# Both directions of a delta rule advanced side by side, and conditioning products on four column groups

## The chip, the cores and the metric

One core of a Trainium2 chip runs the whole program in one launch. The metric is the device time of that launch in microseconds (us). PE is TensorE, DVE VectorE, ACT ScalarE, POOL GpSimd, SP SyncE, whose queue issues the loads.

## The reference

Two blocks follow each other, on 512 latent and 256 context tokens of width 1024, in float32. The first block:

```python
mod = silu(c) @ mod_w + mod_b            # likewise for c_ctx: "conditioning"
p = (layer_norm(x) * (1 + sc) + sh) @ w_in
pv, u, fh, g = split(p)
y = rwkv(shift3(u_ctx), shift3(u_lat))   # 6 heads of 64, two directions
o = hgrn(fh_ctx, fh_lat)                 # 6 heads of 64, two directions
mix = concat(pool(pv), y, o) * silu(g)
x = layer_norm(ALPHA * x + gate * (mix @ w_out)) * ln_g + ln_b
```

The delta rule of `rwkv` runs forward and backward over the tokens, the context first, and per token t it computes

```python
sa = S @ kk_t
S = S * w_t - outer(sa, kk_t * a_t) + outer(v_t, k_t)
y_t = S @ r_t                            # latent tokens only; y of both directions is added
```

The second block (a gated delta net, an attention layer, two feed-forward layers) also takes conditioning products, `silu(c_2) @ ada_w_2`, 2 x 6144 columns. The change does not touch the rest of it.

## The kernel before, in words

Data lie feature-major: tiles of 128 features by tokens. Float32 accuracy of the large products comes from splitting both factors in a high and a low part (`dense`, L272: three products each). Tile's scheduler puts every engine's instructions in one fixed order ahead of the run; dense and conditioning products are placed around the serial chains.

`block1` has two parts. In the first (the opening), 8 loads of 384 KB bring x, `layer_norm` takes sums (L344, `mv`), and `ada` computes the first conditioning group (L311, bank `mi`, 12 load buffers). In the second a loop over n in 0 to 5 takes one piece of `rwkv_pair`, one of `hgrn_pair` and a group of `ada` (bank `ma`, 3 load buffers), then gates and the output product follow.

`ada` multiplies 32 condition columns by a group of 2048 weight columns: for each k of 8 and each of nb = 4 blocks b, a 128x512 tile (256 KB, L310) is loaded and multiplied into rows 32b to 32b+31 of one bank (L311). A float32 matmul leaves two records in the trace. 32 such products are in the opening, 208 in the loop (six groups with nb = 4, one with nb = 2).

`rwkv_pair(p)` (p = 0, 1, 2: two heads) projects k, v, r and calls `rwkv_unit(p, dd)` for each direction dd, so six units run one behind the other. A unit prepares decays and scaled keys (L672 to L728), and then goes through its 12 chunks of 64 tokens in two halves of 6. For each half `rwkv_pre` takes scores on PE (L758), masks them on DVE (L761), and inverts unit triangular blocks of 32 by 32 in `inv32`: 15 rounds of shuffle, product and difference on DVE (L831, L832, L833), from L826 to the transpose of L853, with one merge of 16 to 32; then a merge to 64 (L788 to L807). Each of 6 `rwkv_chunk` steps is a chain: products on PE (L865, L866), a copy on ACT (L870), PE (L872), DVE (`uv`, L873), PE (L875), and the state update `rS` on DVE (L877). The decayed state `pe` (L862) is on ACT. Scores `scs`, transposed keys `bkt`, values `uv` and inverse `tt` lie in the pool `f2`, with two buffers, so a half can be prepared while the other's steps run. `rwkv_out` (L892, L893) multiplies out late. HGRN units begin at L987 (`hlf`) on DVE and end at L946 (`hoa`) for every second of them.

Of the kernel before, what the change touches and what calls it, by code (L numbers as in the profile page):

```python
# [192 lines left out]
class B:  # L193
# [108 lines left out]
    def ada(self, s, c0, w, g, nb, out, bias, st="m"):  # L302
# [10 lines left out]
        ev = pool.tile([128, 512], F32, tag="raw", name="adaev", bufs=nr)  # L313
# [106 lines left out]
    def block1(self):  # L420
# [6 lines left out]
        with tc.tile_pool(name="b1a", bufs=2) as pool, self.banks(mv=6, mi=2), self.stream("i", 12, 1):  # L427
# [13 lines left out]
        with ExitStack() as ctx:  # L441
# [23 lines left out]
            self.late, self.last = None, {}  # L465
# [3 lines left out]
            for n in range(6):  # L469
                next(rw, None)  # L470
# [22 lines left out]
            self.late()  # L493
# [118 lines left out]
    def rwkv_pair(self, p):  # L612
# [26 lines left out]
        last = self.late

        def readout():

            last()
# [14 lines left out]
        self.late = readout  # L658

    def rwkv_unit(self, p, dd, r, k, v, kk, y, pb):  # L660

        nc, tc = self.nc, self.tc
        f1 = self.f1
        col = dd * 3 + p
        P64 = slice(64 * dd, 64 * dd + 64)
        th = {}
        for nm, src, up, hb in (("w", self.xw, self.wup, "rwkv_w0"), ("a", self.xa, self.aup, "rwkv_a0")):
            t = f1.tile([128, NT], F32, tag="t" + nm, name="t" + nm)
            for c0, cn in (LAT, CTX):
                o = self.mm()  # L670
                nc.tensor.matmul(o[:, :cn], up[P64, 128 * p:128 * p + 128], src[P64, c0:c0 + cn], start=True, stop=True)
                nc.vector.tensor_scalar(t[:, c0:c0 + cn], o[:, :cn], self.V(hb, col), SIG_MIN, op0=ALU.add, op1=ALU.max)  # L672
            self.sigmoid(t)
            th[nm] = t
        lw, ta = th["w"], th["a"]
        g = f1.tile([128, 12, 64], F32, tag="G", name="G")
        self.cumsum(g.rearrange("p c t -> p (c t)"), lw, 64, dd)
        e = lw.rearrange("p (c t) -> p c t", t=64)
        nc.scalar.activation(e, g, AF.Exp, scale=CDEC)
        nc.scalar.activation(g, g, AF.Exp, scale=-CDEC)  # L680
        en = g
        end = 63 if dd == 0 else 0
        ec = self.f2.tile([128, 12], F32, name="rec")
        nc.gpsimd.tensor_copy(ec, e[:, :, end])
        kkv = kk.rearrange("p (c t) -> p c t", t=64)
        rv = r.rearrange("p (c t) -> p c t", t=64)

        halves = ((0, 1, 2), (3, 4, 5)) if dd == 0 else ((0, 1, 5), (2, 3, 4))
        ars = []
        for cps in halves:  # L690
            ar = self.ar[self.arn % 3]
            self.arn += 1
            ars.append(ar)
            runs = [(2 * cps[0], 6, 0)] if cps[2] - cps[0] == 2 else [(0, 4, 0), (10, 2, 4)]
            for c, n, q in runs:
                for h in range(2):
# [8 lines left out]
                    lo = max(c, 4)
                    if lo < c + n:
                        nc.gpsimd.tensor_tensor(ar[H, q + lo - c:q + n, h, 1, :], e[H, lo:c + n], rv[H, lo - 4:c + n - 4],
                                                op=ALU.mult)

        bk = f1.tile([128, 6, 4, 64], F32, tag="BK", name="BK")  # L710
        km = f1.tile([128, NT], F32, tag="km", name="km")
        nc.vector.tensor_scalar(km, ta, self.V("rwkv_k_a", p), self.ka[:, p:p + 1], op0=ALU.mult, op1=ALU.add)
        nc.vector.tensor_tensor(km, km, k, op=ALU.mult)
        env = en.rearrange("p (c q) t -> p c q t", q=2)
        nc.vector.tensor_tensor(bk[:, :, 0:4:3, :], km.rearrange("p (c q t) -> p c q t", q=2, t=64), env, op=ALU.mult)
        nc.vector.tensor_tensor(ta, ta, kk, op=ALU.mult)

        tav = ta.rearrange("p (c q t) -> p c q t", q=2, t=64)
        for q in range(2):
            nc.vector.tensor_tensor(bk[:, :, 1 + q, :], tav[:, :, q], env[:, :, q], op=ALU.mult)  # L720
        if dd == 0:
            nc.vector.scalar_tensor_tensor(pb, km[:, 256:], self.V("rwkv_r_k", p), r, op0=ALU.mult, op1=ALU.mult)
        else:
            nc.vector.scalar_tensor_tensor(km[:, 256:], km[:, 256:], self.V("rwkv_r_k", 3 + p), r, op0=ALU.mult, op1=ALU.mult)
            nc.gpsimd.tensor_tensor(pb, pb, km[:, 256:], op=ALU.add)
            bs = self.mm()
            nc.tensor.matmul(bs, self.C("bones"), pb, start=True, stop=True)
# [17 lines left out]
    def rwkv_pre(self, cps, dd, bk, ar, v):  # L745
# [30 lines left out]
        if self.late:  # L776
            self.late()
# [938 lines left out]
```

## Time and profile before

| | |
|---|---|
| median of 3 runs | 2768.44 us (2766.35 to 2769.46) |
| the profiled execution | 2766.63 us, span 2764.8 us |
| busy of the span | PE 2609.9 us (94%), DVE 1687.3 (61%), ACT 1294.9 (47%), POOL 290.4 (11%) |
| block 1 | 0 to 876.5 us of the span |
| state updates L877 | 72, from 173.4 to 860.5 us |

A busy share is an average over the span, and PE's ends are modelled, so a busy PE isn't PE at its peak. Times in a window table are counted from the span's start; "PEclk" is the granted clock of TensorE, 1.00 being full speed. Idle time of an engine is put down to what released it last.

### The profile page before, as it was taken

What the parts mean: (1) busy time and instruction counts of PE and PEld (TensorE: products, weight loads), DVE (VectorE), ACT (ScalarE), POOL (GpSimd) and SP (SyncE); (2) the same over time, 40 slices, a digit from 0 to 9 for tenths busy, and PEclk for the clock granted to TensorE, in tenths of its full rate; (3) what the DMA queues carried; (4) which work ended last, traced back from release to release, by engine and by line L of the source; (5) the groups of instructions that cost most, each with busy time, mean ns of one, the idle gap of its engine ahead of it and who ended that gap; (6) DMA issues with size and microseconds to landing.
All of it is one profiled execution on the core that took longest, in us unless ns stands there. A gap on an engine that the chain in (4) does not pass through costs nothing.

```text
span 2764.8 us, 50823 instructions
## 1 busy us (share of the span) xinstructions
PE 2609.9 (94%) x19688; PEld 1987.2 (72%) x19688; DVE 1687.3 (61%) x4379; ACT 1294.9 (47%) x2927; POOL 290.4 (11%) x387
## 2 busy tenths in 40 slices
PE   8999999999988989999889999999998999999998
PEld 3754645564545777777777888888887788888888
DVE  3676576677666657777766444244454677664665
ACT  2454354546455565555444332133344555543444
POOL 0120021012103001111210110011000000010010
PEclk9999999999989999999989999999999999999999
DMA  5234143323434220111131222222231012233225
GB/s 188 77 100 129 58 138 100 116 62 108 135 92 153 81 71 33 35 37 40 61 102 41 68 65 61 62 64 65 76 110 47 28 29 86 81 96 97 98 90 157
DMA packets 130083, 230.91 MB, mean 84 GB/s; under 512 B 14768, under 2 KB 30384, under 8 KB 129840
## 3 DMA queue, kind: packets, MB, share of 16 engines
q1 hardware_dynamic: 129840, 227.65, 26.7%
q8 instruction: 154, 2.52, 0.4%
q14 instruction: 89, 0.73, 0.1%
HBM read 217.90 MB, written 9.70 MB: 82 GB/s over the span
## 4 chain that ended last, share of the span: by engine, by line
PE 46%; DVE 2%; ACT 1%; issue 1%; POOL 1%; DMA 0%; POOLq 0%; DVEq 0%; SPq 0%; ACTq 0%
PE mm L272 39%; PE ms L1670 2%; PE mv L344 1%; PE mt L1689 1%; PE mt L1683 1%; PE mm L1620 1%; PE mf L272 0%; DVE hl L416 0%; DVE ht L414 0%; DVE wlo L259 0%; POOL qr L1604 0%; POOL qr L1603 0%; ACT whi L258 0%; DMA raw<-ffn_up 0%; ACT hh L415 0%
## 5 line engine op out<-in xcount | busy, mean ns | idle before, releaser
L259 DVE TENSOR_TENSOR wlo<-raw,whi 128x512 fp32r<-128x512 f32 (+3 forms) x560 | 387.2, 693 | 368.5 <-ACT whi L258 224.6
L258 ACT CAST whi<-raw 128x512 fp32r<-128x512 f32 (+3 forms) x560 | 331.7, 594 | 467.8 <-PE mm L272 409.5
L272 PE MATMUL mm<-hh,whi 128*128 128x512 f32 (+1 forms) x1960 | 480.4, 358 | 22.6 <-ACT hh L415 13.3
L272 PE MATMUL mm<-hl,whi 128*128 128x512 f32 (+1 forms) x1960 | 456.4, 349 | 0.1
L272 PE MATMUL mm<-hh,wlo 128*128 128x512 f32 (+1 forms) x1960 | 452.1, 348 | 0.4 <-DVE wlo L259 0.4
L272 PEld LDWEIGHTS mm<-hh,whi 128*128 128x128 f32 x1960 | 330.6, 191 | 87.8 <-ACT hh L415 21.2
L272 PEld LDWEIGHTS mm<-hl,whi 128*128 128x128 f32 x1960 | 327.8, 192 | 48.3 <-issue 5.1
L272 PEld LDWEIGHTS mm<-hh,wlo 128*128 128x128 f32 x1960 | 326.5, 192 | 48.1 <-issue 5.4
L311 PE MATMUL ma<-raw,cvs 128*32 128x512 f32 x416 | 178.6, 620 | 8.4 <-DMA raw<-ada_w 7.1
L1168 POOL TENSOR_TENSOR fc<-fc,fc 128x768 f32<-128x768 f32 (+1 forms) x44 | 69.2, 1572 | 867.6 <-DVE fc L582 635.0
L272 PE MATMUL mm<-fh,whi 128*128 128x256 f32 (+1 forms) x616 | 136.2, 340 | 1.0 <-ACT fh L391 1.0
L580 DVE SCALAR_TENSOR_TENSOR fc<-mm,vec,fc 128x511 f32<-128x511 f32 (+1 forms) x132 | 86.8, 658 | 79.9 <-ACT fc L579 79.9
L272 PE MATMUL mm<-fl,whi 128*128 128x256 f32 (+1 forms) x616 | 130.5, 330 | 0.0
L272 PE MATMUL mm<-fh,wlo 128*128 128x256 f32 (+1 forms) x616 | 129.3, 328 | 0.0
L579 ACT ACTIVATE fc<-mm,vec 128x512 f32<-128x512 f32 (+1 forms) x132 | 81.4, 617 | 96.5 <-PE mm L272 96.4
L272 PEld LDWEIGHTS mm<-fh,whi 128*128 128x128 f32 x616 | 99.9, 190 | 15.7 <-issue 3.4
L272 PE MATMUL mf<-hh,whi 128*128 128x512 f32 (+1 forms) x360 | 103.2, 385 | 5.6 <-ACT whi L258 2.9
L1132 DVE SCALAR_TENSOR_TENSOR xr<-mm,m,xr 128x512 f32<-128x512 f32 (+1 forms) x112 | 66.4, 596 | 67.6 <-PE mm L272 67.6
L272 PEld LDWEIGHTS mm<-fl,whi 128*128 128x128 f32 x616 | 99.0, 190 | 11.3 <-issue 0.5
L272 PEld LDWEIGHTS mm<-fh,wlo 128*128 128x128 f32 x616 | 98.6, 190 | 10.5
L272 PE MATMUL mf<-hl,whi 128*128 128x512 f32 (+1 forms) x360 | 96.4, 368 | 0.0
L344 PE MATMUL mv<-sq,con 128*128 128x256 f32 (+1 forms) x240 | 84.9, 453 | 11.9 <-ACT sq L348 11.5
(539 smaller groups left out, 4483.3 us busy)
## 6 DMA issues: line engine op xcount, KB each, us to landing
raw<-ada_w SPq DMA_DIRECT2D x192, 256.0 KB, 3.0
raw<-ffn_up SPq DMA_DIRECT2D x176, 256.0 KB, 2.6
raw<-ffn_down SPq DMA_DIRECT2D x96, 256.0 KB, 2.7
raw<-w_in SPq DMA_DIRECT2D x66, 256.0 KB, 3.0
raw<-ab_w_in SPq DMA_DIRECT2D x50, 256.0 KB, 2.8
raw<-mod_w SPq DMA_DIRECT2D x48, 256.0 KB, 3.8
raw<-ffn_down SPq DMA_DIRECT2D x48, 192.0 KB, 2.4
raw<-w_out SPq DMA_DIRECT2D x32, 256.0 KB, 2.9
```

The source lines that it names most:

```text
L258: nc.scalar.copy(hi[:, :nk], raw[:, :nk])
L259: nc.vector.tensor_tensor(lo[:, :nk], raw[:, :nk], hi[:, :nk].bitcast(F32), op=ALU.subtract)
L272: nc.tensor.matmul(o, a[:, k], b[:, k0 + k, t:e], start=(k0 == 0 and j == 0 and k == 0), stop=(k0 + n == nk and j == 2 and k == n - 1))
L311: nc.tensor.matmul(acc[32 * b:32 * b + 32, :], s[:, k, :], t, start=(k == 0), stop=(k == 7))
L344: self.nc.tensor.matmul(v[:, :x.shape[1]], self.C("ones"), x, start=(k == 0), stop=(k == 7))
L579: nc.scalar.activation(out[:, c0:c0 + cn], o[:, :cn], AF.Copy, scale=w[1])
L580: nc.vector.scalar_tensor_tensor(out[:, c0 + 1:c0 + cn], o[:, :cn - 1], w[0], out[:, c0 + 1:c0 + cn], op0=ALU.mult, op1=ALU.add)
L1132: nc.vector.scalar_tensor_tensor(x, o[:, :cn], gcol(m, 0 if c0 else 1), x, op0=ALU.mult, op1=ALU.add)
L1168: nc.gpsimd.tensor_tensor(g, g, u, op=ALU.mult)
L1620: nc.tensor.matmul(o[:, e], a[:, k, T], b[:, k], start=(i == 0), stop=(i == 5))
L1670: nc.tensor.matmul(o[:, at:at + cn], a, b, start=(j == 0), stop=(j == 4))
L1683: nc.tensor.transpose(tp[:, j], p[:, (c0 + j) * 128:(c0 + j + 1) * 128], self.C("ident"))
```

## The change

1. `ada` goes through its 512 columns in two halves c; per k one load brings 256 columns of all nb blocks (512 KB for nb = 4, in runs of 1 KB where there were 2 KB), and four products of 256 columns, on four column groups, stand next to each other. Load buffers: 6 in the opening instead of 12, still 3 in the loop, of twice the size.
2. `rwkv_unit` is replaced. `rwkv_prep` prepares both directions; then three sets g of 4 chunks per direction follow. `rwkv_pre(g)` takes the scores of both directions; all blocks are inverted by one `inv8` (8 blocks of 32 by 32 in four row groups; direction 0's are transposed so that both have the same triangle): 7 rounds, then two merge levels. `scs`, `bkt` and `uv` move to `f1`, one buffer each; the inverse `tt` is one fixed tile.
3. `rwkv_chunk` makes a step of both directions, 36 in all: `pe` on POOL, products side by side, `uv` on DVE for direction 0 and on ACT for 1, and two updates. `rwkv_out` runs right behind a set.
4. The loop takes two pieces of `rwkv_pair` for even n and one for odd n.

The second block keeps `inv32`. The diff's core:

```diff
     def ada(self, s, c0, w, g, nb, out, bias, st="m"):
...
-        for k in range(8):
-            for b in range(nb):
-                t = pool.tile([128, 512], F32, tag="raw", name="raw", bufs=nr)
-                nc.sync.dma_start(t, w[k * 128:(k + 1) * 128, g * 2048 + b * 512:g * 2048 + b * 512 + 512])
-                nc.tensor.matmul(acc[32 * b:32 * b + 32, :], s[:, k, :], t, start=(k == 0), stop=(k == 7))
+        for c in (0, 256):
+            for k in range(8):
+                t = pool.tile([128, 4, 256], F32, tag="raw", name="raw", bufs=nr)
+                nc.sync.dma_start(t[:, :nb], w[k * 128:(k + 1) * 128, g * 2048:g * 2048 + nb * 512]
+                                  .rearrange("p (b n) -> p b n", b=nb)[:, :, c:c + 256])
+                for b in range(nb):
+                    nc.tensor.matmul(acc[32 * b:32 * b + 32, c:c + 256], s[:, k, :], t[:, b], start=(k == 0), stop=(k == 7))
...
-        with tc.tile_pool(name="b1a", bufs=2) as pool, self.banks(mv=6, mi=2), self.stream("i", 12, 1):
+        with tc.tile_pool(name="b1a", bufs=2) as pool, self.banks(mv=6, mi=2), self.stream("i", 6, 1):
...
             for n in range(6):
-                next(rw, None)
+                for _ in range(2 - n % 2):
+                    next(rw, None)
                 next(hg)
...
+        bk, ec = self.rwkv_prep(p, r, k, v, kk, pb)
+        yield
...
+        for g in range(3):
+            pre = self.rwkv_pre(g, bk, v)
+            sts = []
+            for i in range(4):
+                sts.append(st)
+                st = self.rwkv_chunk(g, i, ec[:, :, 4 * g + i], pre, st)
+            if g:
+                self.rwkv_out(g, sts, pre, y)
...
+        scs = f1.tile([128, 2, 2, 2, 2, na, 64], F32, tag="scs", name="scs", padded_shape=[128, 2, 2, 2, 2, 2, 64])
+        bkt = f1.tile([128, 2, 2, 2, 128], F32, name="bkt")
+        uv = f1.tile([128, 2, 2, 2, 128], F32, name="uv")
...
+    def inv8(self, c32, U):
...
+        nc.vector.tensor_tensor(x, c32, bc("d8"), op=ALU.mult)
+        for n, o in zip(("o8", "o16"), offs):
+            nc.gpsimd.tensor_tensor(o, c32, bc(n), op=ALU.mult)
...
+        for j in range(7, 0, -1):
+            W = slice(j, 8)
+            nc.vector.stream_shuffle(sh[:, :, W], x8[:, :, W], [8 * b + j for b in range(4) for _ in range(8)])
+            nc.vector.tensor_tensor(pr[:, :, W], sh[:, :, W], a[:, :, j:j + 1].broadcast_to([128, U, 8 - j]), op=ALU.mult)
+            nc.vector.tensor_tensor(x8[:, :, W], x8[:, :, W], pr[:, :, W], op=ALU.subtract)
...
+        for o in offs:
+            nc.vector.transpose(flat(t), flat(x))
...
+                        nc.tensor.matmul(ps[R, n, u], l[R, u], r[R, u], start=True, stop=True, tile_position=(32 * i, 32 * i))
...
+            nc.vector.tensor_tensor(x, x, ps[:, 1], op=ALU.subtract)
...
+    def rwkv_chunk(self, g, i, ec, pre, st):
...
+        nc.gpsimd.tensor_tensor(pe, st, ec.rearrange("p (d o) -> p d o", o=1).broadcast_to([128, 2, 64]), op=ALU.mult)
         ch = self.psum("rch", (128, 4, 128))
...
+            for dd, j, q, b in at:
+                nc.tensor.matmul(ch[b, 0, H[h]], scs[:, dd, j, q, h, 0], uv[:, dd, j, q, H[h]], start=True, stop=False)
+            for dd, j, q, b in at:
+                nc.tensor.matmul(ch[b, 0, H[h]], self.ar[g][dd][:, 2 * j + q, h, 0], st[:, dd], start=False, stop=True)
...
+            if dd == 0:
+                nc.vector.tensor_scalar(uv[b, dd, j, q], ch[b, 1], -1.0, None, op0=ALU.mult)
+            else:
+                nc.scalar.activation(uv[b, dd, j, q], ch[b, 1], AF.Copy, scale=-1.0)
...
+            nc.vector.scalar_tensor_tensor(st2[:, dd], ch[:, 2, H[dd]], ec[:, dd:dd + 1], pe[:, dd], op0=ALU.mult, op1=ALU.add)
```

How the change moves instructions, at three places. First PE at its start, where `mv` are the sums of layer norm and `mi` the conditioning products, before:

```order
L344 MATMUL mv<-x_92,con 128x512 x8
L311 MATMUL mi<-raw,cvs 32x512 x3
L344 MATMUL mv<-sq,con 128x512
L311 MATMUL mi<-raw,cvs 32x512
L344 MATMUL mv<-sq,con 128x512
L311 MATMUL mi<-raw,cvs 32x512 x2
L344 MATMUL mv<-sq,con 128x512
L311 MATMUL mi<-raw,cvs 32x512
```

and now:

```order
L351 MATMUL mv<-x_92,con 128x512 x8
L318 MATMUL mi<-raw,cvs 32x256 x4
L351 MATMUL mv<-sq,con 128x512
L318 MATMUL mi<-raw,cvs 32x256 x4
L351 MATMUL mv<-sq,con 128x512
L318 MATMUL mi<-raw,cvs 32x256 x4
L351 MATMUL mv<-sq,con 128x512 x2
L318 MATMUL mi<-raw,cvs 32x256 x4
```

Lone products and pairs have become sets of four of half the width, each behind a product of the sums.

Second DVE in the second head pair of the program before, where one half's inverse (`rx`, `rpr`, `rsh`) meets the other's steps (`uv`, `rS`):

```order
L831 STREAM_SHUFFLE rsh<-rx_4500 128x6x5
L832 TENSOR_TENSOR rpr<-rsh,ra_4499 128x6x5
L833 TENSOR_TENSOR rx_4500<-rx_4500,rpr 128x6x5
L831 STREAM_SHUFFLE rsh<-rx_4500 128x6x6
L832 TENSOR_TENSOR rpr<-rsh,ra_4499 128x6x6
L833 TENSOR_TENSOR rx_4500<-rx_4500,rpr 128x6x6
L873 TENSOR_SCALAR uv<-rch 64x128
L831 STREAM_SHUFFLE rsh<-rx_4500 128x6x7
L832 TENSOR_TENSOR rpr<-rsh,ra_4499 128x6x7
L877 SCALAR_TENSOR_TENSOR rS<-rch,rec,pe 128x64
L833 TENSOR_TENSOR rx_4500<-rx_4500,rpr 128x6x7
```

and now, at the end of one inverse:

```order
L846 STREAM_SHUFFLE rsh<-rx_2815 128x8x7
L847 TENSOR_TENSOR rpr<-rsh,ra_2814 128x8x7
L848 TENSOR_TENSOR rx_2815<-rx_2815,rpr 128x8x7
L849 TENSOR_TENSOR rx_2809<-rx_2815,con_382 128x256
L854 STREAM_TRANSPOSE rt_2810<-rx_2809 128x256
L846 STREAM_SHUFFLE rsh<-rx_4277 128x8
L864 TENSOR_TENSOR rx_2809<-rx_2809,rsc 128x256
L854 STREAM_TRANSPOSE rt_2810<-rx_2809 128x256
L321 COPY adaev<-ma 128x512
L327 TENSOR_TENSOR m_70<-ma,vec 128x16 x2
L864 TENSOR_TENSOR rx_2809<-rx_2809,rsc 128x256
L865 STREAM_TRANSPOSE rt_2810<-rx_2809 128x256
```

The steps are gone from between the rounds; the rounds end with merge levels that wait for PE (`rsc`).

Third DVE at the last steps of the last head pair and the start of the last HGRN unit (`hlf`, `hg`, `hlv`), before:

```order
L831 STREAM_SHUFFLE rsh<-rx_9225 128x6x8
L873 TENSOR_SCALAR uv<-rch 64x128
L832 TENSOR_TENSOR rpr<-rsh,ra_9224 128x6x8
L987 SCALAR_TENSOR_TENSOR hlf<-hz,hg 128x768
L877 SCALAR_TENSOR_TENSOR rS<-rch,rec,pe 128x64
L833 TENSOR_TENSOR rx_9225<-rx_9225,rpr 128x6x8
L593 SCALAR_TENSOR_TENSOR hg<-con,hlf 128x128
L831 STREAM_SHUFFLE rsh<-rx_9225 128x6x9
L593 SCALAR_TENSOR_TENSOR hg<-con,hlf 128x128
L832 TENSOR_TENSOR rpr<-rsh,ra_9224 128x6x9
```

and now:

```order
L937 TENSOR_SCALAR uv<-rch 64x128
L945 SCALAR_TENSOR_TENSOR rS<-rch,rec,pe 128x64 x2
L937 TENSOR_SCALAR uv<-rch 64x128
L945 SCALAR_TENSOR_TENSOR rS<-rch,rec,pe 128x64 x2
L399 TENSOR_TENSOR hl<-gb,hh 128x512 x2
L937 TENSOR_SCALAR uv<-rch 64x128
L1052 SCALAR_TENSOR_TENSOR hlf<-hz,hg 128x768
L945 SCALAR_TENSOR_TENSOR rS<-rch,rec,pe 128x64 x2
L596 SCALAR_TENSOR_TENSOR hg<-con,hlf 128x128 x6
```

The last HGRN unit stood ahead of 10 of the last unit's updates, and stands now ahead of those of two steps.

## Rows read from the trace of the kernel before

**Rows 1.** Windows of the span: window, its length, busy us (records) of PE, PEld, DVE, ACT, POOL, PEclk, DMA share, GB/s.

```profile
0.00:58.00 58.00, 47.73 (x132) 15.04 (x132) 11.69 (x26) 15.04 (x27) 2.45 (x11) 0.99 0.65 220
58.00:173.50 115.50, 105.21 (x608) 76.30 (x609) 81.36 (x218) 60.56 (x115) 20.46 (x35) 0.93 0.24 78
173.50:860.50 687.00, 647.05 (x7546) 362.75 (x7545) 469.30 (x1700) 347.43 (x1117) 97.08 (x186) 0.98 0.35 105
860.50:876.50 16.00, 8.21 (x144) 3.79 (x143) 8.58 (x20) 8.10 (x30) 4.62 (x4) 0.89 0.67 217
876.50:2764.80 1888.30, 1801.72 (x11260) 1529.33 (x11260) 1116.35 (x2418) 863.75 (x1640) 165.83 (x151) 0.98 0.23 71
```

**Rows 2.** Windows by steps and gaps, and idle time ahead of L877, by its releaser.

```profile
173.50:199.50 26.00, 25.74 (x155) 12.98 (x154) 17.70 (x73) 10.79 (x26) 4.36 (x5) 1.00 0.41 132
199.50:219.50 20.00, 14.86 (x319) 9.70 (x317) 16.11 (x64) 11.19 (x45) 3.65 (x10) 0.74 0.11 28
...
307.50:317.80 10.30, 10.30 (x193) 7.74 (x194) 4.17 (x14) 4.28 (x11) 0.83 (x2) 1.00 0.17 53
...
337.50:440.00 102.50, 96.27 (x969) 47.03 (x968) 78.33 (x242) 62.04 (x179) 20.52 (x37) 1.00 0.41 124
...
622.80:693.20 70.40, 63.74 (x871) 34.74 (x867) 56.08 (x198) 45.02 (x151) 14.88 (x24) 0.98 0.35 110
...
842.90:860.60 17.70, 16.76 (x369) 11.22 (x361) 14.62 (x44) 11.58 (x48) 3.49 (x5) 1.00 0.21 62
...
L877 DVE SCALAR_TENSOR_TENSOR rS<-rch,rec,pe x72: 267/283/285, 173.4 to 860.5; 128x64 f32<-128x64 f32 x72
...
  PE rch L875: 19.0, 29
```

**Rows 3.** Lines L826 and L853 (start and end of an inverse): first and last start.

```profile
L826 DVE TENSOR_SCALAR ra<-rc,con x12: 253/631/643, 141.4 to 802.8; 128x96 f32<-128x96 f32 x12
...
L853 DVE STREAM_TRANSPOSE rt<-rx x12: 359/378/379, 164.4 to 833.3; 128x192 f32<-128x192 f32 x12
```

**Rows 4.** Timeline of DVE: two rounds' shuffles; lines of DVE, 58 to 877 us: preparation.

```profile
449.34 0.20 DVE L831 STREAM_SHUFFLE rsh<-rx 128x30 f32<-128x30 f32 x1
...
450.04 0.20 DVE L831 STREAM_SHUFFLE rsh<-rx 128x36 f32<-128x36 f32 x1
...
L593 DVE TENSOR_TENSOR_SCAN G<-con,tw 128x64 f32<-128x64 f32 x72 | 14.7, 269 | 1.7 <-ACT tw L332 1.6
...
L713 DVE TENSOR_TENSOR km<-km,rk 128x768 f32<-128x768 f32 x6 | 5.7, 950 | 0.1
```

**Rows 5.** Windows, line L311 alone (PE, PEld); a PE line of 60 to 890 us.

```profile
0.00:58.00 58.00, 20.78 (x64) 2.91 (x64) 0.99 0.65 220
58.00:877.00 819.00, 178.59 (x416) 23.65 (x416) 0.97 0.34 103
...
L865 PE MATMUL rch<-uv,scs 128*64 128x64 f32 x288 | 40.7, 235 | 1.0 <-DVE rS L877 1.0
```

**Rows 6.** Timeline of PE in the opening: start, length, records.

```profile
25.34 1.04 PE L311 MATMUL mi<-raw,cvs 128*32 128x512 f32 x2
...
27.37 1.06 PE L311 MATMUL mi<-raw,cvs 128*32 128x512 f32 x6
...
52.20 1.90 PE L311 MATMUL mi<-raw,cvs 128*32 128x512 f32 x10
```

**Rows 7.** DMA from 868 to 886 us, GB/s in 40 slices.

```profile
GB/s 0 86 50 237 360 400 405 419 405 405 423 396 387 391 362 373 346 348 350 344 357 357 371 387 387 387 391 178 18 0 0 91 323 314 323 155 155 314 146 178
```

**Rows 8.** Line L987, the start of an HGRN unit.

```profile
L987 DVE SCALAR_TENSOR_TENSOR hlf<-hz,hg x6: 937/945/959, 186.1 to 811.6; 128x768 f32<-128x768 f32 x6
```

**Rows 9.** Timelines of POOL and of DVE around 461 us.

```profile
460.72 1.01 POOL L707 TENSOR_TENSOR AR<-tw,rr 64x384 f32<-64x384 f32 x1 [0.88 <-PE rsc L892]
...
460.76 1.06 DVE L832 TENSOR_TENSOR rpr<-rsh,ra 128x72 f32<-128x72 f32 x1
...
462.42 0.24 DVE L832 TENSOR_TENSOR rpr<-rsh,ra 128x78 f32<-128x78 f32 x1
```

More of the change, by code (lines that the diff above doesn't have):

```diff
@@ L656, in readout, with rwkv_prep @@
                 nc.sync.dma_start(self.ymix[:, 2 + p], y)
-        self.late = readout
-    def rwkv_unit(self, p, dd, r, k, v, kk, y, pb):
-        nc, tc = self.nc, self.tc
+        readout()
+    def rwkv_prep(self, p, r, k, v, kk, pb):
+        nc = self.nc
         f1 = self.f1
[L664 to L684, printed above, removed]
@@ L705, in rwkv_unit @@
[L705 to L713, printed above, removed]
@@ L714, in rwkv_unit @@
[L714 to L718, printed above, removed]
-        for q in range(2):
[L720 to L727, printed above, removed]
-            nc.vector.tensor_tensor(pb, bs, v[:, 256:], op=ALU.mult)
@@ new lines, in rwkv_pre @@
+        Q = [slice(32 * i, 32 * i + 32) for i in range(4)]
+        quads = [(dd, slice(4 - 4 * dd, 8 - 4 * dd), 2 * b + dd, 2 * b + 1 - dd, *((x, t) if dd == 0 else (t, x)))
+                 for dd in range(2) for b in range(2)]
+        for u in range(4):
+            for dd, U, s, e, x_, t_ in quads:
+                nc.tensor.matmul(ps[Q[e], 0, U.start + u],
+                                 scs[Q[s], dd, u // 2, 1 - s // 2, u % 2, 0, 32 * (e % 2):32 * (e % 2) + 32],
+                                 t_[Q[s], U.start + u], start=True, stop=True, tile_position=(32 * s, 32 * e))
@@ new lines, in rwkv_pre @@
+        for dd, U, s, e, x_, t_ in quads:
+            (nc.vector.tensor_copy if s > 1 else nc.scalar.copy)(w[Q[e], U], ps[Q[e], 0, U])
+        for u in range(4):
+            for dd, U, s, e, x_, t_ in quads:
+                nc.tensor.matmul(ps[Q[s], 1, U.start + u], w[Q[e], U.start + u], x_[Q[e], U.start + u],
+                                 start=True, stop=True, tile_position=(32 * e, 32 * s))
+        for dd, U, s, e, x_, t_ in quads:
+            q = 1 - s // 2
+            for z in (s, e):
+                nc.scalar.copy(tt[Q[z], U, q, 32 * (z % 2):32 * (z % 2) + 32], x_[Q[z], U])
@@ new lines, in rwkv_chunk @@
+        xs = self.f1.tile([128, 128], F32, name="xs", bufs=2)
+        nc.scalar.copy(xs, ch[:, 0])
+        for h in range(2):
+            for dd, j, q, b in at:
+                nc.tensor.matmul(ch[b, 1, H[h]], self.tt[:, 4 - 4 * dd + 2 * j + h, q], xs[:, H[h]], start=True, stop=True)
+        for dd, j, q, b in at:
+            if dd == 0:
+                nc.vector.tensor_scalar(uv[b, dd, j, q], ch[b, 1], -1.0, None, op0=ALU.mult)
+            else:
+                nc.scalar.activation(uv[b, dd, j, q], ch[b, 1], AF.Copy, scale=-1.0)
@@ L899, in rwkv_out @@
-        return emit
+                    nc.tensor.matmul(yp[H, T], st[:, dd], self.ar[g][dd][:, 2 * j + q, h, 1, :], start=True, stop=False)
+                    nc.tensor.matmul(yp[H, T], uv[:, dd, j, q, H], scs[:, dd, j, q, h, 1, :], start=False, stop=True)
+        if g == 1:
+            nc.scalar.copy(y, yp)
+        else:
+            nc.vector.tensor_tensor(y, yp, y, op=ALU.add)
     def hgrn_lb(self):
```

302 lines of the change are left out of this document (162 added, 140 removed).

## The prediction

> **What bounds the kernel now.** I read the profile from the coarse to the fine. The stretches come first [rows 1]: block 1 is everything up to 876.5 us, and the 1888.3 us after it run code that the change does not touch, so they enter the sum unchanged. Within block 1, the opening of 58.0 us (layer norm and the first conditioning products) has PE busy for 47.73 us. From the first dense product to the first state update of the delta rule pass 115.5 us, from there to the last update 687.0 us with PE busy for 647.05, and 16.0 us are left behind it. PE looks like the bound. But its queue is filled with dense and conditioning products that were placed around the serial chain of the delta rule, so a busy PE alone does not say which of the two sets the end.
>
> The view by steps tells more. The state update (L877) runs 72 times, in twelve stretches of six, and between two stretches a gap [rows 2]. The stretches take 26.0 us at first and 17.7 us at last; all twelve hold 60 step intervals in 264 us, 4.4 us each. The rest, 423 us, are eleven gaps: those within a unit from 10.3 us up, the two between head pairs 102.5 and 70.4 us. Every gap is preparation: scores, and the inverse of a triangular block, whose start (L826) and end (L853) are in [rows 3]. Its 15 rounds on DVE follow each other at 0.7 us (450.04 − 449.34) and can't be shortened by another engine [rows 4]. So steps and gaps add up, and PE's products must fit in.
>
> **The opening.** The conditioning products (`ada`) of the opening are 32, in 64 records, 20.78 us of PE [rows 5]. A lone one takes 1.04 us (2 records), three on different column groups together 1.06 (6 records), and five 1.90, of which two must share a group [rows 6]. So products on different column groups run at the same time. The change issues 16 sets of four half-width products; a set should take half of a lone product, 0.52 us, 8.3 us in all, 12.5 us less on PE. Then the loads decide: at 220 GB/s the first 58 us carry 12.8 MB [rows 1], about 11.9 MB of it ahead of the first dense product (32 loads of 256 KB, 8 of 384 KB, the constants). The change halves the contiguous runs from 2 to 1 KB; in the row of 868 to 886 us the 2 KB part runs at some 400 GB/s, the part of 1 KB runs at 345 to 357 [rows 7]. 11.9 MB at 350 GB/s are 34 us, plus 2 us to the first landing, plus the 3.9 us from the end of the last products (54.1 [rows 6]) to the first dense one (58.0): 40 us at best, 46 if layer norm is late. I take 43: **−15 us**, ends −18 and −8.
>
> **To the first update.** The unit's preparation is now done for both directions ahead of any step. On DVE one direction is nine groups from the scan's 14.7 us down to 5.7 us, 71.5 us over six units, so 12 us each [rows 4]. The first inverse of 23 us [rows 3] has 7 rounds instead of 15, −6 us, and a second merge level on PE adds a little; fewer score columns give 2. **+4 us**, ends −5 and +12.
>
> **Steps.** 36 steps instead of 72, each with both directions, and 27 intervals within sets. I take 4.4 us for an interval: PE's products of the two directions stand in different halves of the array, the decay product leaves ScalarE for POOL, where it isn't on the chain, and a second update of 0.28 us follows the first. 27 × 4.4 = 119 us. Ends 3.5 (17.7/5) and 5.2 (26.0/5): 96 to 140 us.
>
> **Gaps.** Nine sets make eight gaps. Two are between pairs, where both directions' preparation, the readout and projections now sit: before, 102.5 us with DVE busy 78.33 and 70.4 with 56.08 [rows 2]. The new order puts about 88 and 83 us of DVE work there. The old ratio (1.31 and 1.26) would give 115 and 104 us; but in the old gaps PE was 94% and 91% busy, and it loses conditioning work, so I take 102 and 92: 194 us, ends 175 and 220.
>
> The six gaps within pairs are the new weak point. Scores, transposed keys and values are single-buffered, so the inverse of the next set can't start beside the steps of this one; formerly it did, which is why a gap could be 10.3 us. The chain alone: the shortest inverse of 23 us − 6 + 4 (second merge level), with scores and copies ahead and the block merge behind it at 4 us each, about 30 us. Two gaps hold little else: 30 each. Two with HGRN work on both PE and DVE I put at 50, the other two at 38 and 42, from the work the order places there (33 to 43 us on the busiest engine). Sum 240 us, ends 180 (all at the chain) and 300 (all at 50).
>
> So first to last update is 119 + 194 + 240 = 553 us against 687.0: **−134**.
>
> **Conditioning in block 1b.** Its 416 records are 178.59 us of PE [rows 5], 0.86 us a product. In the new order the 416 half-width products stand in 109 runs between other products, 54 of them shorter than four; counted four at a time that makes 137 slots. At 0.52 us a slot they cost 71 us, at 0.86 us 118; I take 0.6 us, 82 us, 97 less. This isn't a term of its own: it is what lets the gaps be as short as taken above.
>
> **Tail.** The last HGRN unit used to start at 811.6 us [rows 8], 49 us ahead of the last update, and ended at the end of block 1, 876.5 [rows 1], 65 us later. Now it starts two steps ahead of the last update and is exposed: 65 us less 10 that it overlaps, 55 us instead of 16.0: **+39**, ends +25 and +49.
>
> **POOL.** At 460.72 us POOL multiplies for 1.01 us; a DVE product started at 460.76 takes 1.06 us, its like 1.7 us later 0.24 [rows 9]. So a POOL read delays a round by up to 0.8 us. The change adds on POOL two masks an inverse and 36 decay products. At 0.8 us each that is 54 × 0.8 = 43 us at most and nothing at least. I take nothing: the decay product starts a step and is wanted at its end, and DVE waits for PE in a step anyway (19.0 us before L877 alone [rows 2]); the masks run while the first rounds do and are wanted behind them. The Trainium skill, page "SBUF — State Buffer", section "Who interferes with whom", says that a DVE instruction with two SBUF inputs and a GpSimd one that reads SBUF lock each other out. Row and rule agree; taken strictly, every such pair on the path, the rule would give 2703 us.
>
> **Sum.** −15 + 4 − 134 + 39 = −106 on a profiled execution of 2766.6 us (span 2764.8), which stands 1.8 us under the median of 2768.4: 2660.6, so **2660 us**.
>
> **Rivals.**
> A, the forecast: the chain of steps and gaps decides, 2630 to 2700 us. For it: steps and gaps add up in [rows 2]; chance 0.55.
> B: block 1 follows PE. Its 760.5 us of PE in the 818.5 from 58.0 to 876.5 [rows 1] are 93%. Less 97 (conditioning) and some 33 (a fifth of four groups of step products, the largest 40.7 us [rows 5], standing side by side) 631 remain, at 93% 678 us: −140, with the opening −155, 2611 us. For it: the busy share. Against: the new serial inverses leave PE without work. Chance 0.22.
> C: products side by side only in the opening, where loads are ahead. With 512 KB loads in three buffers and runs of 1 KB, a set waits for its load, splits, and most of the 97 us stay; where PE is the busiest, about two thirds of the gaps, 60 us come back: 2720 us. For it: the 54 short runs. The Trainium skill, page "TensorEngine Tiling (Array Packing)", section "Key Properties", says that a change of tiling mode drains the engine; before, each lone product was such a change too, and its 0.86 us of busy time stood inside 1.04 us elapsed. Chance 0.15.
> D, slower: the single buffers. If every in-pair gap lasts 58 us instead of 40, the 106 us are gone (106/6 = 18 each); at 65 us the time is 2810. For it: the last inverse, with other work placed between its rounds, took 30.5 us against 23.0 for the first [rows 3], and the stretch from 199.5 to 219.5 shows a granted clock of 0.74 [rows 2], so PE idle in serial inverses may cost more: it took 20.0 us where another gap of its kind took 10.3, and 3 us more in each of nine sets would be 27 us. Against: those had twice the rounds. Chance 0.05.
> That the change does nothing, its parts cancelling, 2761 to 2772 us, has 0.03.
>
> **Numbers.** The measurement tells about 0.2% (5.5 us). Faster is A, B and C, 0.92; same 0.03; slower 0.05. The ends of the terms add to −234 and +26 if all fell together, which they need not, so the range takes B at its lower side and C: **2595 to 2725 us**, leaving some 0.18 outside.
>
> **What would show it.** Right: first dense product near 43 us; conditioning near 82 us of PE; 27 intervals of 4.4 us; in-pair gaps of 30 to 50 us; the last HGRN unit alone behind the last update; the rest at 1888 us. Wrong: conditioning still above 130 us (C), in-pair gaps of 58 us and more (D), or gaps that shrink to PE's work with PE above 90% (B); a changed rest would make all of it wrong.

## The result, and the profile after

The changed kernel takes 2732.26 us (median of 4 runs, 2724.74 to 2736.78) against 2768.95; the ratio is 0.9869 with a 95% interval of 0.9854 to 0.9884. It is faster, as forecast, but by 37 us where 106 were forecast, and above the range of 2595 to 2725 us. The profiled execution is the slowest of the four, 2736.8 us (span 2735.0).

The windows of the span after, as in [rows 1]: opening, to the first update, to the last one, tail, rest.

```profile
0.00:46.40 46.40, 35.36 (x197) 14.59 (x197) 11.32 (x25) 15.20 (x28) 0.80 (x7) 1.00 0.84 275
46.40:176.50 130.10, 112.09 (x825) 79.72 (x826) 85.86 (x181) 56.66 (x102) 26.47 (x45) 0.91 0.24 76
176.50:798.50 622.00, 546.79 (x8518) 351.62 (x8516) 378.03 (x1115) 315.74 (x968) 114.50 (x215) 0.90 0.36 113
798.50:845.70 47.20, 26.52 (x523) 14.60 (x523) 30.38 (x82) 25.50 (x104) 11.01 (x14) 0.57 0.29 94
845.70:2735.00 1889.30, 1802.96 (x11260) 1530.00 (x11260) 1115.74 (x2417) 863.79 (x1640) 166.52 (x151) 0.97 0.23 71
```

| term | forecast | measured |
|---|---|---|
| opening (58.0) | 43, −15 | 46.4, −11.6 |
| to the first update (115.5) | +4 | 130.1, +14.6 |
| 27 step intervals | 119 | 129.2 |
| two gaps between pairs | 194 | 230.6 |
| six gaps within pairs | 240 | 261.9 |
| first to last update (687.0) | 553, −134 | 622.0, −65 |
| tail (16.0) | 55, +39 | 47.2, +31.2 |
| rest (1888.3) | 0 | 1889.3, +1.0 |
| sum | −106 | −29.8 of span |

The windows by steps and gaps, as in [rows 2]. The first line is a set of four steps, the others are gaps: the second and third follow the first and the second set of the first pair, 305.60 and 551.40 stand between pairs, the rest are gaps of the other two pairs.

```profile
176.70:191.20 14.50, 13.62 (x144) 9.11 (x144) 6.47 (x17) 8.34 (x19) 3.67 (x7) 1.00 0.31 93
191.20:228.90 37.70, 28.27 (x694) 19.27 (x690) 28.48 (x106) 24.39 (x94) 5.47 (x13) 0.73 0.23 72
...
244.70:291.80 47.10, 43.83 (x700) 26.98 (x696) 23.10 (x76) 18.11 (x52) 7.53 (x16) 1.00 0.54 168
...
305.60:423.50 117.90, 96.72 (x1245) 62.37 (x1244) 83.81 (x214) 63.39 (x175) 25.55 (x46) 0.87 0.32 102
...
437.30:462.40 25.10, 24.42 (x484) 18.06 (x481) 14.30 (x51) 11.30 (x31) 4.02 (x7) 1.00 0.37 118
...
476.50:537.90 61.40, 55.96 (x1063) 34.55 (x1059) 38.54 (x128) 36.03 (x140) 10.03 (x18) 0.89 0.46 142
...
551.40:664.10 112.70, 93.88 (x1214) 56.03 (x1214) 80.50 (x207) 60.67 (x170) 26.57 (x47) 0.83 0.38 120
...
678.20:706.80 28.60, 26.41 (x467) 19.08 (x465) 12.91 (x49) 10.46 (x28) 3.46 (x6) 0.88 0.23 77
...
721.50:783.50 62.00, 51.20 (x1049) 30.79 (x1042) 38.40 (x127) 34.47 (x136) 7.22 (x17) 0.86 0.39 121
```

The steps are there, 4.8 us each. But the gaps are not short of work: DVE is busy for 84 of 118 and 81 of 113 us between pairs, and the granted clock, 0.98 in [rows 1] from first to last update, is 0.90, down to 0.73 in a gap, and 0.57 in the tail.

How PE comes to idle and lose its clock shows between the second and the third pair. First its timeline, then windows of 4 us.

```profile
590.27 2.77 PE L318 MATMUL ma<-raw,cvs 128*32 128x256 f32 x18
594.93 0.64 PE L318 MATMUL ma<-raw,cvs 128*32 128x256 f32 x8 [1.90 <-DMA raw<-ada_w]
596.36 0.64 PE L318 MATMUL ma<-raw,cvs 128*32 128x256 f32 x8 [0.79 <-DMA raw<-ada_w]
604.69 1.62 PE L763 MATMUL rsc<-AR,BK 128*128 128x128 f32 x6 [7.69 <-DVE BK L727]
```

```profile
592.00:596.00 4.00, 1.68 (x14) 0.31 (x9) 4.00 (x17) 2.67 (x5) 0.98 (x2) 0.80 0.79 262
596.00:600.00 4.00, 0.64 (x8) 0.16 (x8) 3.93 (x7) 3.37 (x9) 3.82 (x5) 0.62 0.00 0
600.00:604.00 4.00, 0.00 (x0) 0.00 (x0) 3.97 (x5) 0.00 (x0) 1.92 (x3) 0.50 0.22 66
604.00:608.00 4.00, 2.37 (x7) 1.86 (x8) 4.00 (x6) 0.49 (x3) 2.29 (x2) 0.50 0.43 131
608.00:612.00 4.00, 3.93 (x18) 2.04 (x16) 3.99 (x10) 1.28 (x7) 2.22 (x2) 0.67 0.45 131
612.00:616.00 4.00, 3.80 (x112) 2.55 (x112) 3.86 (x16) 1.82 (x8) 0.42 (x2) 1.00 0.83 244
```

PE waits 7.69 us for DVE, which is busy throughout with the preparation of the second direction (HGRN's stands in between up to 595.7 us), until the keys (`BK`, L727) are scaled; the conditioning group is at its end by then. The clock is at half from 600 to 608 and back at full from 612. The Trainium skill, page "TensorE: Matmul & The Clock Gate", section "Why this matters for your kernels", advises against idle gaps between bursts of products, because the clock drops behind them; the rows agree.

The same work at a lower clock is dearer on PE. A set of four conditioning products takes 0.64 us at full clock (594.93 above) and 1.08 at half (638.79). HGRN's products, whose code is unchanged, before:

```profile
L1047 PE MATMUL mf<-sct,hit 128*64 128x128 f32 x96 | 21.3, 307 | 5.5 <-ACT sct L1034 5.0 <-ACT sct L1039 0.5
L1046 PE MATMUL mf<-hqe,hS 128*64 128x128 f32 x96 | 20.8, 317 | 4.0 <-ACT sct L1039 3.7 <-issue 0.2
```

and after, with the conditioning (178.59 us in [rows 5]) and the merge products of the new inverse:

```profile
L318 PE MATMUL ma<-raw,cvs 128*32 128x256 f32 x832 | 95.6, 427 | 15.3 <-DMA raw<-ada_w 10.6 <-DMA raw<-mod_w 2.9 <-ACT sct L1099 1.6
...
L1112 PE MATMUL mf<-sct,hit 128*64 128x128 f32 x96 | 27.1, 375 | 11.1 <-ACT sct L1099 11.0
L1111 PE MATMUL mf<-hqe,hS 128*64 128x128 f32 x96 | 25.0, 366 | 10.7 <-ACT sct L1104 8.6 <-DVE hrd L1096 1.7 <-issue 0.3
...
L861 PE MATMUL rsc<-rt,ro 32*32 32x32 f32 x1152 | 15.7, 202 | 3.0 <-DVE rsh L846 1.7 <-DVE rt L854 0.8 <-issue 0.5
L861 PE MATMUL rsc<-rx,rw 32*32 32x32 f32 x1152 | 15.0, 201 | 1.7 <-issue 1.7
```

The products of unchanged code in block 1 (1200 records of dense products and 3030 of HGRN in both traces, summed by the line view) took 476.9 us before and 501.6 after, of which HGRN's rose from 130.3 to 150.2. Of these 4230 records 233 ran below the full clock before and 1066 after; those at full clock cost the same, within 1 us in all, so the increase lies in those below it. This is time of PE; whether the kernel's end moves with it is another question (e2 and e10 below).

### The profile page after: what moved, and what is told of

Its sections match the earlier page's. It is cut to its first block, busy times and chain, and to the rows that moved or that the text cites. A ratio compares the mean times of both kernels' runs of the same rounds, so it can differ in the third digit from the quotient of the medians.

```text
span 2735.0 us, 53289 instructions
## 1 busy us (share of the span) xinstructions
PE 2523.7 (92%) x21320; PEld 1990.5 (73%) x21320; DVE 1621.3 (59%) x3815; ACT 1276.9 (47%) x2840; POOL 319.3 (12%) x432
## 4 chain that ended last, share of the span: by engine, by line
PE 47%; DVE 2%; ACT 2%; issue 1%; POOL 1%; DMA 0%; POOLq 0%; SPq 0%; DVEq 0%; ACTq 0%
PE mm L277 39%; PE ms L1735 2%; PE mt L1754 1%; PE mv L351 1%; PE mt L1748 1%; PE mm L1685 1%; PE mf L277 0%; DVE hl L423 0%; DVE ht L421 0%; POOL qr L1669 0%; ACT hh L422 0%; DMA raw<-mla_w_out 0%; ACT whi L263 0%; ACT qrh L1705 0%; PE mm L1665 0%
## 5 line engine op out<-in xcount | busy, mean ns | idle before, releaser
L318 PE MATMUL ma<-raw,cvs 128*32 128x256 f32 x832 | 95.6, 427 | 15.3 <-DMA raw<-ada_w 10.6
L277 PEld LDWEIGHTS mm<-fh,wlo 128*128 128x128 f32 x616 | 98.6, 190 | 10.4
```

Of the source, the lines that this page charges most:

```text
L277: nc.tensor.matmul(o, a[:, k], b[:, k0 + k, t:e], start=(k0 == 0 and j == 0 and k == 0), stop=(k0 + n == nk and j == 2 and k == n - 1))
L318: nc.tensor.matmul(acc[32 * b:32 * b + 32, c:c + 256], s[:, k, :], t[:, b], start=(k == 0), stop=(k == 7))
```

## The experiments

Every kernel was timed in three rounds beside the kernel before. For each profile the stretch from the first dense product to the end of block 1 is split in PE's busy and idle time. A profile is of one execution, which stands off the median by some us: the changed kernel's by +5, e1's by −5, e9's by +11, e10's by −8, e14's by −9.

| run | median us | ratio [interval] | stretch = busy + idle, us | PEclk |
|---|---|---|---|---|
| before | 2768 to 2770 | | 819.1 = 760.5 + 58.6 | 0.97 |
| changed | 2732.3 | 0.9869 [0.9854, 0.9884] | 799.3 = 685.4 + 113.9 | 0.88 |
| e1 | 2708.8 | 0.9769 [0.9752, 0.9787] | 765.8 = 695.4 + 70.4 | 0.93 |
| e2 | 2768.3 | 0.9994 [0.9979, 1.0009] | 821.0 = 733.6 + 87.4 | 0.95 |
| e3 | 2760.3 | 0.9953 [0.9933, 0.9972] | 824.7 = 732.1 + 92.6 | 0.95 |
| e4 | 2744.0 | 0.9901 [0.9883, 0.9919] | 806.3 = 697.1 + 109.2 | 0.87 |
| e5 | 2741.9 | 0.9901 [0.9885, 0.9918] | 810.6 = 732.7 + 77.9 | 0.96 |
| e6 | 2717.5 | 0.9817 [0.9802, 0.9833] | 784.0 = 689.1 + 94.9 | 0.88 |
| e7 | 2791.8 | 1.0084 [1.0067, 1.0101] | 834.5 = 754.1 + 80.4 | 0.96 |
| e9 | 2737.2 | 0.9893 [0.9867, 0.9919] | 812.1 = 733.9 + 78.2 | 0.91 |
| e10 | 2707.5 | 0.9773 [0.9750, 0.9797] | 763.5 = 652.9 + 110.6 | 0.90 |
| e11 | 2751.9 | 0.9943 [0.9924, 0.9962] | 818.9 = 725.4 + 93.5 | 0.89 |
| e12 | 2718.1 | 0.9811 [0.9790, 0.9832] | 781.1 = 695.5 + 85.6 | 0.91 |
| e13 | 2707.7 | 0.9783 [0.9768, 0.9798] | 769.8 = 671.2 + 98.6 | 0.93 |
| e14 | 2725.7 | 0.9841 [0.9820, 0.9862] | 779.8 = 678.5 + 101.3 | 0.91 |
| e15 | 2712.9 | 0.9798 [0.9776, 0.9820] | 771.1 = 667.2 + 103.9 | 0.87 |

**Which part gains: e1, e2, e3.** e1 is the kernel before with the new `ada`; e2 the changed one with the old `ada`; e3 has the old one in the loop alone (`ada_lone`).

```diff
-                self.ada(s, 2, d["ada_w"][l], g, 4, self.m2[l][:, 16 * g:16 * g + 16],
+                self.ada_lone(s, 2, d["ada_w"][l], g, 4, self.m2[l][:, 16 * g:16 * g + 16],
```

> The kernel before with the new conditioning products alone (sets of four, opening and loop); the delta rule as it was. Chain theory (steps and gaps of the delta rule set the end, products fill in): only the opening's 12 us are won, 2757 us, and PE in the loop falls from 178.6 to some 95 us with more idle time and a lower granted clock. PE theory (block 1 follows PE's work): 12 and most of 83 us, 2680 to 2700 us.

> The changed kernel with the old conditioning products (lone ones of 512 columns), so the new delta rule alone. Chain theory: the opening's 12 us come back and little else, 2744 to 2755 us, with a granted clock above 0.90 from first to last update because PE has more to do. PE theory: 12 and 83 us come back, 2827 us, slower than the kernel before.

> The changed kernel with lone products in the loop, and sets of four in the opening. Clock theory (PE idles behind the preparation, its clock is halved and that costs what the smaller work saved): 2725 to 2740 us, granted clock from first to last update 0.94 or more. PE theory: 2815 us.

The conditioning alone brings 61 us, of which the opening has 11 (first dense product at 47.2 us). The new rule alone brings nothing, and on top of the new conditioning it costs 23 us. So for the kernel before the PE theory is the nearer one (9 us outside its range; the chain theory is 48 us off): PE's busy time fell by 65 us and the stretch by 53, with the delta rule untouched. The chain itself waits for PE there: its 60 step intervals fell from 264 to 235 us and its gaps from 423 to 403. Neither theory foretold e2: the rule takes 27 us off PE's busy time, and PE idles 29 us more. Nor did either foretell e3: the clock from first to last update rose to 0.96, as its clock theory had it, and yet the time is 2760 us, not 2725 to 2740. Under the new rule the loop's sets are worth 28 us (e3 against the changed kernel), under the old one some 50 (61 less 11). With both parts new, PE has less to fill its waits with, and idles 55 us more than before. The row of e2 from first to last update shows it beside [rows 1]: 642.3 us instead of 687.0, yet 127.9 to the first update and 50.8 in the tail.

```profile
56.70:184.60 127.90, 114.79 (x806) 79.39 (x807) 83.04 (x181) 56.33 (x102) 26.52 (x45) 0.92 0.25 81
184.60:826.90 642.30, 581.04 (x8099) 333.03 (x8097) 383.55 (x1113) 315.44 (x972) 120.31 (x217) 0.97 0.33 103
826.90:877.70 50.80, 37.74 (x545) 15.12 (x545) 28.80 (x83) 24.45 (x101) 8.00 (x12) 0.75 0.49 157
```

The two gaps between pairs in e2, to be held against 305.60 and 551.40 above:

```profile
320.90:440.10 119.20, 102.56 (x1163) 53.64 (x1163) 83.96 (x212) 60.70 (x171) 26.06 (x46) 1.00 0.36 112
577.70:692.10 114.40, 99.04 (x1136) 51.15 (x1135) 82.63 (x208) 62.52 (x173) 27.38 (x47) 0.97 0.36 114
```

With lone products 65 us of PE in these two gaps are conditioning, with sets of four 31 us; the clock is 1.00 and 0.97 instead of 0.87 and 0.83. The gaps take 233.6 us in all, and 230.6 in the changed kernel. At full clock, in the first of them, PE is idle for 17 of 119 us, so its work does not set the length there; and the 34 us that left the gaps with the sets of four shortened them by 3. Whether the lower clock took a part of that back the rows do not tell.

**POOL: e4.** Decay product on ScalarE, masks on DVE.

```diff
-        nc.gpsimd.tensor_tensor(pe, st, ec.rearrange("p (d o) -> p d o", o=1).broadcast_to([128, 2, 64]), op=ALU.mult)
+        for dd in range(2):
+            nc.scalar.activation(pe[:, dd], st[:, dd], AF.Copy, scale=ec[:, dd:dd + 1])
...
-            nc.gpsimd.tensor_tensor(o, c32, bc(n), op=ALU.mult)
+            nc.vector.tensor_tensor(o, c32, bc(n), op=ALU.mult)
```

> The changed kernel with the decay product of a step on ScalarE (two of 0.27 us for one of 0.52 us) and the two masks of an inverse on DVE. If POOL's reads, which block DVE, hold the chain: 15 to 40 us faster, 2692 to 2717 us, steps of 4.2 us instead of 4.8 and shorter in-pair gaps. If not: 2725 to 2745 us, with steps within 0.2 us of 4.8.

12 us slower by the medians, though the intervals of the two ratios just touch (0.9884 and 0.9883): the 27 intervals grew from 129.2 to 144.7 us, the gaps shrank from 492.5 to 485.1. Both moves were made at once, so what is shown is that together they bring nothing; what the lock between POOL and DVE costs by itself stays open.

**Serial sets: e5, e7.** Both on e3's base, where there is room. e5 gives the scores a second buffer; e7 emits the next pair's preparation ahead of the last set's steps, and for its room takes one of the loop's three load buffers for conditioning.

```diff
-        scs = f1.tile([128, 2, 2, 2, 2, na, 64], F32, tag="scs", name="scs", padded_shape=[128, 2, 2, 2, 2, 2, 64])
+        scs = f1.tile([128, 2, 2, 2, 2, na, 64], F32, tag="scs", name="scs", bufs=2, padded_shape=[128, 2, 2, 2, 2, 2, 64])
```

```diff
             pre = self.rwkv_pre(g, bk, v)
+            if g == 2:
+                nxt = self.rwkv_front(p + 1) if p < 2 else None
```

> The kernel of e3 (new rule, lone products in the loop, 2760 us) with two buffers for the scores, so that the scores and the inverse of a set can run beside the steps of the set before it. If the single buffer makes the in-pair gaps (273 us in e3 between the last update of a set and the first of the next): the four first gaps of the pairs shrink from 27 to 44 us to 10 to 25 us, with somewhat longer steps, 2715 to 2740 us. If the gaps are what DVE and PE have to do there anyway: the gaps' loss comes back as longer steps, 2755 to 2765 us.

> The kernel of e3 (2760 us) with the next pair's preparation emitted ahead of the last set's steps, with a second tile for that set's AR and for the bonus; two load buffers for the conditioning in the loop instead of three. If preparation in front of the first scores is the loss between pairs (119 us each in e3): these gaps fall to 85 to 100 us, the last sets' steps grow by 10 to 15 us each, 2725 to 2745 us. If DVE's work as such sets them: within 8 us of 2760.

e5 is 18 us faster than e3, so on this base a part of the loss is the single buffer: the pairs' first gaps fell to 20.6, 17.0 and 19.8 us, from 43.7, 28.0 and 27.0, while the second ones grew by 9 to 12 us. e7 is 31 us slower. Its gaps between pairs did fall, to 70 and 80 us, but the second gaps of the first two pairs rose to 87 and 83 us (48 and 66 in e3) and the intervals to 180.7 us (136.4): DVE's preparation met the next inverse instead. But block 1 holds only 10 of the 25 us between the two profiles. The other 15 lie behind it, where the last conditioning products stand until 899 us (854 in e3), several of them waiting 0.4 to 3.2 us for a load; so much of e7's loss may be the missing load buffer, and the run tells nothing sure of the early preparation as such.

**HGRN's place: e6.**

```diff
-                for _ in range(2 - n % 2):
+                for _ in range(1 + n % 2):
```

> The changed kernel with the pieces of the loop in another turn: one of the delta rule for even n and two for odd n. If the last HGRN unit, alone behind the last update (47 us at a granted clock of 0.57), and HGRN's preparation on top of the delta rule's are the loss: the tail falls to under 25 us, the two gaps between pairs from 118 and 113 to about 100, 2690 to 2715 us. If the delta rule's chain carries the end and HGRN fills it: the tail's gain comes back as longer gaps, 2725 to 2740 us.

15 us faster. The tail fell to 9.0 us, and first to last update grew to 646.6: the exposed unit was a loss, but two thirds of the 38 us saved on it were lost again, as longer gaps.

**The inverse: e9, e10.** e9 is e1 with the new inverse, e10 the changed kernel with the old one on its 8 blocks.

```diff
-        x, t = self.inv8(c32[:, 0:2].rearrange("p d u t -> p (d u) t"), 8)
+        x, t = self.inv32(c32[:, 0:2].rearrange("p d u t -> p (d u) t"), 8, 0, self.f1, "r", "rsc")
```

> The kernel of e1 (old rule, new conditioning, 2709 us) with the new inverse alone: 7 rounds and two merge levels for one half's 6 blocks, where there were 15 rounds and one. If the rounds on DVE are on the path: 8 rounds of 0.7 us less 4 us for the merge, twelve times, part of it hidden: 10 to 25 us faster, 2684 to 2699 us. If halves are covered by the other half's steps, or the merge level costs as much on PE: 2703 to 2715 us.

> The changed kernel with the old inverse (15 rounds, one merge level) on its 8 blocks, all else as changed. If e9's loss of 28 us came from the inverse's second merge level, which puts 18 us more work on PE: the 8 more rounds take 9 x 6 us of DVE, but PE gets the 18 us back, 2715 to 2740 us. If the rounds are on the chain of the serial gaps and PE is not the bound: 9 x 6 us less 9 x 3 us for the merge, 27 us slower, 2755 to 2770 us.

The new inverse costs 28 us in the old rule and 25 in the new one. Two gaps of e10, the second pair's, against 437.30 and 476.50 above, and its merge products:

```profile
423.40:454.20 30.80, 29.88 (x402) 20.68 (x400) 21.99 (x89) 15.58 (x37) 2.70 (x7) 1.00 0.43 139
...
469.00:517.80 48.80, 45.17 (x796) 30.10 (x797) 37.47 (x134) 30.46 (x112) 6.35 (x15) 1.00 0.40 126
...
L907 PE MATMUL rsc<-rx,rw 32*32 32x32 f32 x576 | 7.3, 199 | 0.9 <-issue 0.9
L907 PE MATMUL rsc<-rt,roff 32*32 32x32 f32 x576 | 7.1, 198 | 7.0 <-DVE rsh L889 5.7 <-DVE rt L900 1.2
```

Where a gap holds little else, the 8 rounds cost what they should, 30.8 us against 25.1. Where HGRN runs beside the inverse, the gap is 48.8 us instead of 61.4, PE is busy for 45.17 instead of 55.96 us, and the clock stays at 1.00. Over the whole stretch PE's busy time falls by 32 us: the merge products take 7.1 + 7.3 us instead of 15.7 + 15.0, which is 16 of them, and unchanged code fell from 501.6 to 469.3 us. That is less than the 476.9 before, at a granted clock of 0.90 against 0.97, so this sum does not follow the clock alone. The short inverse did shorten the inverses: from the first DVE operation of each to its last transposition the nine take 206 us, and 229 in e10. But the two beside HGRN (third sets of the second and third pair) take 33.7 and 31.0 us, and 22.1 and 22.3 in e10. PE's waiting is not the difference: e10 waits for `BK` for 22.0 us, the changed kernel for 18.3, and both idle alike (110.6 and 113.9 us). How the cost divides between the products themselves and the hand-overs of a second level (DVE, PE, ACT, PE, DVE) no run separates.

**The clock: e12, e13, e14, e15.** 24 useless products while DVE prepares, in the changed kernel (e12), of 32 columns instead of 512 (e14), and of 512 in e10 (e13). e15 is e10 with e6's turn.

```diff
             nc.scalar.activation(en, en, AF.Exp, scale=-CDEC)
+            for _ in range(4):
+                fill = self.mm()
+                nc.tensor.matmul(fill, self.C("bones"), en.rearrange("p c t -> p (c t)")[:, 0:512], start=True, stop=True)
```

> The changed kernel with 24 useless products of 512 columns (1.04 us each at full clock, 25 us in all), which read the decays of a direction's preparation and whose results nothing reads, so that PE works while DVE prepares. If PE's idle stretches there cost clock: granted clock over block 1 above the changed kernel's 0.88, the same products of unchanged code (504 us in the changed kernel, 481 before) fall to under 497, and the time stays within 8 us of 2732 in spite of 25 us more work. If the clock does not matter there and PE is the bound: 2750 to 2760 us.

> The changed kernel with 24 useless products at e12's places and with its dependences, but of 32 columns instead of 512, so with a sixteenth of the work. If e12 gained by PE's work while DVE prepares, through the clock: no gain here, 2727 to 2737 us. If it gained by the other order that the added instructions bring about: 2713 to 2723 us.

> e10 (changed kernel with the old inverse, 2707.5 us) with e12's 24 useless products of 512 columns. If PE's idle stretches in the preparation cost clock there too: 8 to 15 us faster again, 2692 to 2700 us. If the short inverse was what brought the clock down: within 5 us, or slower by up to 20 us for the added work.

> e10 (2707.5 us) with e6's turn of the pieces. If the exposed HGRN unit (37 us behind the last update in e10) is a loss of its own: 10 to 15 us faster, 2692 to 2698 us. If the short inverse beside HGRN was what e6 helped: 2703 to 2712 us.

e12 is 14 us faster with 24.3 us more work on PE; the wait for `BK` fell from 18.3 to 4.9 us in block 1, the clock rose to 0.91, unchanged code fell only to 495.3 us. The gain does not stand where the useless products do, ahead of the first update and in the two gaps between pairs:

```profile
300.50:419.10 118.60, 102.95 (x1261) 63.87 (x1260) 84.11 (x213) 62.92 (x175) 24.80 (x46) 0.88 0.34 108
544.20:661.00 116.80, 104.89 (x1262) 62.36 (x1261) 83.71 (x213) 64.58 (x178) 27.66 (x48) 0.93 0.40 130
```

These gaps took 117.9 and 112.7 us without them. What fell are the six gaps within pairs, from 261.9 to 242.9 us, 12 of it in the last one alone. e14, 2725.7 us, lies between the changed kernel and e12, in neither of its two ranges, and its interval meets both. The added rows also move others in the scheduler's order, so how much of the 14 us is the clock stays open. e13, 2707.7 us, is no faster than e10, though its clock is 0.93 instead of 0.90 and its wait for `BK` 4.8 us instead of 22.0; its PE carries 18 us more. e15, 2712.9 us, gains nothing over e10 either: e6's and e12's gains were gains over the short inverse, not beside it.

**Together: e11.** e6's turn, e5's buffer, and 256 KB loads (two column groups each) to make room, with 12 load buffers in the opening instead of 6.

```diff
-                t = pool.tile([128, 4, 256], F32, tag="raw", name="raw", bufs=nr)
+                    t = pool.tile([128, 2, 256], F32, tag="raw", name="raw", bufs=nr)
```

> The changed kernel with e6's turn of the pieces, e5's second buffer for the scores, and conditioning loads of 256 KB in place of 512 KB to make room for it. If the serial sets and the placing of HGRN are two separate losses: 15 and 18 us under the changed kernel's 2732, 2699 us, 2690 to 2708 us, below e1's 2709. If both act on the same loss: 2710 to 2722 us.

Slower by 20 us than the changed kernel. The loads undid the sets:

```profile
L321 PE MATMUL ma<-raw,cvs 128*32 128x256 f32 x832 | 142.8, 446 | 30.8 <-DMA raw<-ada_w 26.6 <-DMA raw<-mod_w 1.9 <-DVE wlo L264 0.9
```

142.8 us where the same 832 records took 95.6: products of two loads mostly run two and two. In the trace of e11 four records of L321 start within 0.15 us of each other 41 times and two 240 times, in the changed kernel's (L318) 134 and 34 times. So the run says nothing of the other two edits together.

## Why the prediction was wrong

- **Opening**: right in kind, 46.4 us against 43, at the forecast's late end.
- **Conditioning in the loop**: 95.6 us against 82 forecast. The error was to call it no term of its own. It is the whole gain: e1, with the old rule, wins 61 us, and e2, with the new rule alone, nothing. So the premise of rival A, that the chain of steps and gaps decides and PE's products fit in, failed; in the kernel before PE comes near to setting the pace (53 us of stretch for 65 of PE in e1), rival B's reason. The sentence "a busy PE alone does not say which of the two sets the end" is true, but I went on as if the chain did.
- **To the first update**, +14.6 against +4: the second direction's preparation is there; the shorter inverse did not pay for it. With the old inverse it is +18.2 (e10).
- **Steps**: 129.2 us against 119, a matter of size.
- **Gaps**: this is the term of the sum that failed, 492.5 us against 434; that is 58 of the 76 us by which the sum missed the span. Between pairs I set 102 and 92 us, below what the old ratio gave (115 and 104), on the ground that PE loses conditioning work. They took 118 and 113, and the ground was wrong: with 34 us more conditioning in them they take 119 and 114, at a clock of 1.00 and 0.97 (e2). DVE's two preparations stand in front of the first scores, with DVE busy for 84 and 81 us as forecast; that they set the gap is argued, not shown by a run that changes them alone. Within pairs I forecast 240 us and 261.9 were measured. The gaps with HGRN took 61.4 and 62.0 us, where I had allowed 50 at most: the 4 us set for the second merge level were wrong there. With the old inverse the six take 239.6 us (e10), the two with HGRN 48.8 and 50.7.
- **Tail**: right in kind, 47.2 us against 55, and avoidable (e6).
- **Rivals**: D's two mechanisms are real, single buffers (18 us in e5, on e3's base) and clock (24.7 us of PE on unchanged code; D named 27 us of time), but they stood in a rival of 0.05 and not in the sum. That the second figure is so near is luck: it is PE's time, and no run shows that the kernel is that much longer for it. C happened in e11, and in the changed kernel only in so far as 95.6 us are more than 82.
- **POOL** at nothing: not contradicted; the stricter reading of the lock, 2703 us in place of 2660, would have moved the forecast the right way for another reason than the one found, since e4 does not get those 43 us back.

What stays open is how the 23 us between e1 and the changed kernel divide into PE's added products, idle time and clock. Shown is that undoing the inverse alone takes them back: e10 keeps the new rule and equals e1, so there too the new rule is worth nothing. Both are 0.9% under the changed kernel and, with e13, the fastest versions found.

## What to carry to other kernels

Test whether a full engine or a chain sets the end by changing one alone before adding up both: here the products that "only filled in" were the gain, and the chain's 36 saved steps were worth nothing. Don't buy a shorter chain on an engine with room with instructions on the fullest one, however small: the shorter inverse, with 31 us of tiny products where the longer one had 14, cost 25 us. Merging two preparations into one puts both in front of the first product that needs them; count what the other engines have left to do meanwhile.

## What the runs showed of the hardware

Twenty-four products that nobody reads, 24.3 us of PE, made one kernel 14 us faster and another no slower (e12, e13); in e12 the gain lies in other places than the products, so it is not shown to be the clock's. A set of four products of 256 columns on four column groups takes 0.64 us (8 records at 594.93), where I had taken 0.52 from half a lone product; two sets back to back take 1.07 (16 records at 41.24), so 0.52 holds only for sets in a row. More than half of what such sets save in the loop is lost when their operands come by two loads instead of one: 178.6, 142.8 and 95.6 us for lone products, e11 (which has two other edits) and the changed kernel.
